# A hybrid decoder layer: triangular inverses on GpSimd, sums of squares in ScalarE's copies, two evacuations on ScalarE

## The chip, the core and the metric

The kernel runs on one core of one Trainium2 chip. The core's engines work beside each other, each through its own queue in order: TensorE (PE in the profile; its weight loads are PEld), VectorE (DVE), ScalarE (ACT), GpSimd (POOL) and SyncE (SP), which here issues the DMAs. The metric is the device time of one execution, in microseconds (us), as the median of several runs.

## What is computed

A layer over 16 meta tokens and 512 tokens of width 1024. RMS normalisation, one wide projection, and then two branches that run side by side: eight heads of differential softmax attention, and eight heads of a gated DeltaNet in chunks. Both are normalised, gated, projected, merged and projected again. What the change touches, cut from the reference:

```python
m = where(strict, einsum(kb, k) * decay, 0.0)                 # per head and chunk
t_inv = triangular_solve(m + eye, eye, lower, unit_diagonal)  # its inverse
v_new = u_c - w_c @ state                                     # u, w come from t_inv
o_c   = qd_c @ state + a_c @ v_new
state = state * cd_c + kd_c.T @ v_new
o_d   = rms_norm(o_d, dn_norm_w)
...
p  = softmax(where(causal, s, -inf))
pd = p[:, :, 0] - lam * p[:, :, 1]
o_a = rms_norm(pd @ v, attn_norm_w) * (1 - lam_init)
```

The kernel takes chunks of 128 tokens for the DeltaNet, and the 16 meta tokens as a first state.

## The kernel before

**The order is planned.** The program is written as many small tasks (Python generators) that say `yield ENGINE` before the instructions for that engine, `yield ("pool",)` where they need a buffer and `yield "event"` where they wait for another task. The class `Plan` (lines 82 to 192) plays the tasks through at build time with a charge for every instruction (`Engine.time`, lines 224 to 251) and for every hop between engines, takes the task that could start first, by rank where two are equal, and so fixes the order of the instructions in every engine's queue. On the chip each engine takes its queue strictly in that order and waits where an input is late. For GpSimd the plan charges `100 + 2.2 * n` nanoseconds for a two-input instruction of n elements per partition that isn't a power (line 250), and no gap between two of them that depend on each other; for VectorE `69 + n / 0.96` and a gap of 130 between dependent ones.

**TensorE's work.** The dense products (`product`, line 737) multiply the normalised tokens, split in two float32r parts (hnH, hnL), with blocks of 128 columns of weights, split likewise (wh, wl): 8 blocks of 128 rows by three passes, over 512 columns, or over two pieces of 272 and 256. Each block of weights is loaded (SP: `raw`), rounded by ACT (`wh`) and its rest taken by DVE (`wl<-raw,wh`, 128x1024, both inputs in SBUF). These products are rank 4 in the plan and fill every place that the heads leave.

**The DeltaNet heads** go in four groups of two (`delta_pair`, line 900). Per group: the products of keys with keys and with queries (lines 1040 and 1041; rows `kT` and `qT,kT` of PE), which DVE scales into MT and AT. The 32x32 diagonal blocks of MT go through DRAM (`scrm`) into msub, where one partition holds one block: 32 blocks of the two heads and one of the meta tokens, twice, in 97 partitions. There the inverse is built by substitution in 31 steps (lines 1166 to 1173), each of two dependent instructions: `tmps<-msub,ts` (a product) and `ts<-ts,tmps` (a difference) on n = 31 - j rows by w = min(j + 1, 16) columns. The result goes through DRAM (`scrt`) to td, and PE takes it up in the row `td,MT` (line 1258), the first of a chain that assembles the inverse TT of 128x128 (`square`), and then runs the four chunks (`steps`, line 1318). PE's queue holds dense products between the last `qT,kT` row of a group and its first `td,MT` row: while the inverse is under way, these keep PE busy.

**The attention heads** (`attention`, line 1405) run in the same stretches: scores into psc, row maxima on DVE, exponentials on ACT, the combination `e<-e,ast,e` on DVE (both inputs in SBUF), transposes into PSUM, copies into pT, the product with the values, and the norm.

**The sums of squares** of the norms: after all four chunks of a head are copied out of PSUM by ACT, ACT squares the 128x512 tile (lines 1372 and 1520) and DVE reduces it (1374 and 1522). **The values** of the DeltaNet are transposed into PSUM, and DVE scales all four chunks in one instruction into vr (line 1001). **The transposed softmax weights** are copied into pT by ACT in every second block of queries and by DVE in the others (lines 1444 to 1449).

GpSimd does little: the masks of E, clearing ts and TT, powers of a few elements, and the DMAs that move half of the keys to other partitions (`ak<-ak`).

## Time and profile before

| | |
|---|---|
| median of 3 runs | 784.66 us (784.42 to 785.24) |
| the profiled execution, its own time | 781.76 us |
| its span, first to last instruction | 780.1 us |
| granted TensorE clock, mean | 0.996 |
| busy: PE, DVE, ACT, POOL | 752.1, 601.7, 410.6, 76.1 us |

The profile is one execution. The page gives the busy time of each engine, the costliest groups of instructions and what ended their waits. `bank<-hnH,wh` is an instruction that writes the PSUM tile bank and reads hnH and wh; nearly all instructions carry one line number, that of the helper that records them, so they are told apart by tiles. The view of waits says which engine waited for which, in total, how often, and longest. The view of stretches gives each engine's busy time between two moments, and the granted clock of TensorE. The timeline lists instructions by start and duration; in brackets stands how long the engine had been idle and what ended that.

### The profile page before, as it was taken

What the parts mean: (1) busy time and instruction counts of PE and PEld (TensorE: products, weight loads), DVE (VectorE), ACT (ScalarE), POOL (GpSimd) and SP (SyncE); (2) the same over time, 40 slices, a digit from 0 to 9 for tenths busy, and PEclk for the clock granted to TensorE, in tenths of its full rate; (3) what the DMA queues carried; (4) which work ended last, traced back from release to release, by engine and by line L of the source; (5) the groups of instructions that cost most, each with busy time, mean ns of one, the idle gap of its engine ahead of it and who ended that gap; (6) DMA issues with size and microseconds to landing.
All of it is one profiled execution on the core that took longest, in us unless ns stands there. A gap on an engine that the chain in (4) does not pass through costs nothing.

```text
span 780.1 us, 14350 instructions
## 1 busy us (share of the span) xinstructions
PE 752.1 (96%) x5479; PEld 688.9 (88%) x5479; DVE 601.7 (77%) x1415; ACT 410.6 (53%) x1000; POOL 76.1 (10%) x114
## 2 busy tenths in 40 slices
PE   5999999999999999998999999899999999999996
PEld 5999878999988899987899998788988998899886
DVE  6788698688669678868967884995697887879643
ACT  5374535676544557654466744355565445545332
POOL 4120002021100201100030201001000000000001
PEclk9999999999999999999999999999999999999999
DMA  8032624212352500254250125223022332332802
GB/s 311 33 110 82 156 82 101 69 38 83 85 153 83 124 29 28 82 143 96 82 123 29 55 84 125 85 86 93 28 82 82 108 110 84 105 101 89 271 0 109
DMA packets 46749, 74.43 MB, mean 95 GB/s; under 512 B 20528, under 2 KB 29136, under 8 KB 46680
## 3 DMA queue, kind: packets, MB, share of 16 engines
q1 hardware_dynamic: 45400, 69.18, 29.0%
q0 software_dynamic: 1280, 4.33, 2.7%
q8 instruction: 43, 0.70, 0.4%
q14 instruction: 26, 0.21, 0.1%
HBM read 65.98 MB, written 3.19 MB: 89 GB/s over the span
## 4 chain that ended last, share of the span: by engine, by line
PE 41%; DMA 4%; DVE 4%; ACT 2%; issue 1%; POOL 1%; SPq 1%; POOLq 0%; ACTq 0%; DVEq 0%
PE bank L220 39%; PE psc L220 1%; DMA msub<-scrm 1%; DMA scrt<-ts 1%; DVE wl L220 1%; DVE ts L220 1%; SPq L220 1%; DVE tmps L220 1%; DMA eg<-gcd 1%; DMA raw<-in_wout_dram 1%; DMA td<-scrt 0%; POOL ts L220 0%; DVE aq L220 0%; ACT wh L220 0%; DVE MT L220 0%
## 5 line engine op out<-in xcount | busy, mean ns | idle before, releaser
L220 PE MATMUL bank<-hnH,wh 128*128 128x512 f32 (+3 forms) x944 | 317.0, 338 | 0.8 <-ACT hnH L220 0.8
L220 PE MATMUL bank<-hnH,wl 128*128 128x512 f32 (+3 forms) x944 | 302.4, 322 | 3.2 <-DVE wl L220 3.2
L220 PE MATMUL bank<-hnL,wh 128*128 128x512 f32 (+3 forms) x944 | 301.8, 322 | 0.0
L220 PEld LDWEIGHTS bank<-hnH,wl 128*128 128x128 f32 x944 | 177.3, 189 | 19.0 <-DVE wl L220 5.1
L220 PEld LDWEIGHTS bank<-hnH,wh 128*128 128x128 f32 x944 | 177.4, 189 | 13.4 <-ACT hnH L220 1.0
L220 PEld LDWEIGHTS bank<-hnL,wh 128*128 128x128 f32 x944 | 177.8, 189 | 10.4
L220 DVE TENSOR_TENSOR wl<-raw,wh 128x1024 fp32r<-128x1024 f32 x82 | 100.1, 1220 | 22.6 <-ACT wh L220 22.2
L220 ACT CAST wh<-raw 128x1024 fp32r<-128x1024 f32 x82 | 85.9, 1048 | 40.8 <-PE bank L220 29.9
L220 DVE SCALAR_TENSOR_TENSOR y<-xp,pc,y 128x528 f32<-128x528 f32 (+1 forms) x72 | 54.2, 754 | 0.8 <-ACT y L220 0.2
L220 ACT ACTIVATE e<-psc,ast 128x144 f32<-128x144 f32 (+3 forms) x64 | 34.5, 541 | 31.8 <-DVE ast L220 27.8
L220 DVE TENSOR_TENSOR tmps<-msub,ts 97x240 f32<-97x240 f32 (+27 forms) x124 | 39.2, 316 | 4.6 <-DMA msub<-scrm 2.9
L220 DVE TENSOR_TENSOR ts<-ts,tmps 97x240 f32<-97x240 f32 (+27 forms) x124 | 39.4, 318 | 1.8
L220 PE MATMUL bank<-btH,Wh 128*128 128x256 f32 x128 | 36.1, 282 | 1.6 <-ACT sn L220 1.6
L220 PE MATMUL bank<-btL,Wh 128*128 128x256 f32 x128 | 35.7, 279 | 0.0
L220 PE MATMUL bank<-btH,Wl 128*128 128x256 f32 x128 | 35.7, 279 | 0.0
L220 PE MATMUL psc<-ak,aq 128*128 128x264 f32 (+3 forms) x160 | 29.1, 304 | 5.8 <-ACT e L220 5.8
L220 PEld LDWEIGHTS psc<-ak,aq 128*128 128x128 f32 x160 | 23.6, 189 | 8.7 <-ACT e L220 7.5
L220 DVE TENSOR_TENSOR Wl<-raw,Wh 128x1024 fp32r<-128x1024 f32 (+1 forms) x24 | 24.8, 1042 | 7.2 <-ACT Wh L220 7.0
L220 ACT CAST Wh<-raw 128x1024 fp32r<-128x1024 f32 (+1 forms) x24 | 21.5, 905 | 16.7 <-DVE raw L220 5.6
L220 POOL DMA_DIRECT2D ak<-ak x16 | 8.8, 551 | 219.6 <-DVE ak L220 160.9
L220 DVE TENSOR_REDUCE ast<-psc 128x1 f32<-128x528 f32 (+3 forms) x40 | 28.4, 710 | 0.2
L220 PEld LDWEIGHTS bank<-btH,Wh 128*128 128x128 f32 x128 | 24.0, 188 | 2.6 <-ACT sn L220 2.2
(339 smaller groups left out, 1466.6 us busy)
## 6 DMA issues: line engine op xcount, KB each, us to landing
raw<-in_wblk_dram SPq DMA_DIRECT2D x96, 512.0 KB, 3.5
ak<-ak POOLq DMA_DIRECT2D x16, 264.0 KB, 4.3
raw<-in_wout_dram SPq DMA_DIRECT2D x8, 512.0 KB, 4.2
xt<-in_x_dram SPq DMA_DIRECT2D x4, 512.0 KB
E<-gcd SPq DMA_DIRECT2D x8, 256.0 KB, 5.0
eg<-gcd SPq DMA_DIRECT2D x8, 256.0 KB
xr<-in_x_dram SPq DMA_DIRECT2D x8, 256.0 KB, 6.8
out_dram<-xr SPq DMA_DIRECT2D x8, 256.0 KB, 2.3
```

Source lines behind the costliest of these rows:

```text
L220: return real(*args, **kw)
```

## The change

Four parts. The 62 instructions of each group's inverse are issued on GpSimd. The squares of the DeltaNet's and the attention's outputs are taken chunk by chunk by ACT straight from PSUM, each behind the copy of the same chunk, with ACT's accumulator giving the sum: the two large squares and the two reduces per head go. The values are scaled by four ACT instructions instead of one of DVE. All copies into pT are ACT's. The memory reserved for descriptors of GpSimd's DMAs is halved, from 4096 to 2048.

```diff
-            yield DVE
-            V.tensor_tensor(out=vr[i], in0=pt, in1=sc[:, i, :, vs_].unsqueeze(2).broadcast_to([P, NC, P]), op=ALU.mult)
+            for c in range(NC):
+                yield ACT
+                A.activation(out=vr[i][:, c, :], in_=pt[:, c, :], func=AF.Copy, scale=sc[:, i, c, vs_:vs_ + 1])
...
         for j in range(31):
             n, w = 31 - j, min(j + 1, 16)
-            yield DVE
+            yield POOL
             tm = mk(dp, [P, 256], F32, "tmps", 2)[0:97, 0:n * w].rearrange("p (i c) -> p i c", c=w)
-            V.tensor_tensor(out=tm, in0=msub[0:97, j, j + 1:32].unsqueeze(2).broadcast_to([97, n, w]),
+            G.tensor_tensor(out=tm, in0=msub[0:97, j, j + 1:32].unsqueeze(2).broadcast_to([97, n, w]),
                             in1=ts_[0:97, j, 0:w].unsqueeze(1).broadcast_to([97, n, w]), op=ALU.mult)
-            yield DVE
-            V.tensor_tensor(out=ts_[0:97, j + 1:32, 0:w], in0=ts_[0:97, j + 1:32, 0:w], in1=tm, op=ALU.subtract)
+            yield POOL
+            G.tensor_tensor(out=ts_[0:97, j + 1:32, 0:w], in0=ts_[0:97, j + 1:32, 0:w], in1=tm, op=ALU.subtract)
...
                     A.copy(out=o[:, c, :], in_=pk[:, 3 * P:4 * P])
+                    A.activation(out=mk(dp, [P, P], F32, "sqk", 1), in_=pk[:, 3 * P:4 * P], func=AF.Square,
+                                 accum_out=co[:, c:c + 1])
                     give("pdl", pk)
...
-            A.activation(out=sq, in_=o, func=AF.Square)
-            yield DVE
-            V.tensor_reduce(out=co, in_=sq, axis=AX.X, op=ALU.add)
...
-            if i % 2:
-                yield ACT
-                A.copy(out=dst, in_=pt[:, :w])
-            else:
-                yield DVE
-                V.tensor_copy(out=dst, in_=pt[:, :w])
+            yield ACT
+            A.copy(out=dst, in_=pt[:, :w])
...
             A.copy(out=o[:, i, :], in_=po[:, 0:P])
+            A.activation(out=mk(ap, [P, P], F32, "sqo", 1), in_=po[:, 0:P], func=AF.Square, accum_out=ss[:, i:i + 1])
             give("pat", po)
...
-        sq = slot(ap, [P, L], F32, "e")[:, :SEQ].rearrange("p (c d) -> p c d", d=P)
-        ss = mk(ap, [P, NC], F32, "ass", 2)
-        yield ACT
-        A.activation(out=sq, in_=o, func=AF.Square)
-        yield DVE
-        V.tensor_reduce(out=ss, in_=sq, axis=AX.X, op=ALU.add)
...
-    nc = _bacc.Bacc("TRN2", target_bir_lowering=False, num_devices=1, dynamic_dma_scratch_size=4096)
+    nc = _bacc.Bacc("TRN2", target_bir_lowering=False, num_devices=1, dynamic_dma_scratch_size=2048)
```

Since the plan sees other charges, the order changes on every engine from the first group on. Three places matter for what follows.

GpSimd's queue where the first group's inverse stands. Before, the mask of E follows the moves of the keys, and then the next tile ts is cleared:

```order
L220 DMA ak_1031<-ak_1031 64x1056 x2
L220 AFFINE_SELECT E_1018<-E_1018 128x512
L220 AFFINE_SELECT E_1085<-E_1085 128x512
L220 DMA ak_1602<-ak_1602 64x1056
L220 MEMSET ts_1605 64x512
L220 AFFINE_SELECT ts_1605<-ts_1605 64x512
```

Now the 62 instructions of the inverse stand there without a break. The first of them:

```order
L220 AFFINE_SELECT E_998<-E_998 128x512
L220 DMA ak_1038<-ak_1038 64x1056
L220 TENSOR_TENSOR tmps_1159<-msub_108,ts_648 97x31
L220 TENSOR_TENSOR ts_648<-ts_648,tmps_1159 97x31
L220 TENSOR_TENSOR tmps_1163<-msub_108,ts_648 97x60
L220 TENSOR_TENSOR ts_648<-ts_648,tmps_1163 97x30x2
```

And the last of them, with what is queued behind: the second mask of E, the clearing of ts and TT, the moves of the next attention head's keys, and the power of the first attention head's norm.

```order
L220 TENSOR_TENSOR tmps_1547<-msub_108,ts_648 97x16
L220 TENSOR_TENSOR ts_648<-ts_648,tmps_1547 97x16
L220 AFFINE_SELECT E_1095<-E_1095 128x512
L220 MEMSET ts_1558 64x512
L220 AFFINE_SELECT ts_1558<-ts_1558 64x512
L220 MEMSET ts_1558 64x512
L220 AFFINE_SELECT ts_1558<-ts_1558 64x512
L220 MEMSET TT_1563 128x1024
L220 MEMSET t_246_1564 32x8x32
L220 DMA ak_1604<-ak_1604 64x1056 x2
L220 TENSOR_TENSOR ass_1282<-ass_1282,mhalf 128x4
```

The mask moved behind the inverse; the moves and the power were there behind the clearing before, too.

VectorE's queue in the middle of the same inverse. Before, its steps alternate with the attention's rows:

```order
L220 TENSOR_TENSOR ts_648<-ts_648,tmps_1311 97x18x14
L220 SCALAR_TENSOR_TENSOR od_132<-th_1309,bank_5_82 128x512
L220 TENSOR_TENSOR tmps_1337<-msub_108,ts_648 97x255
L220 TENSOR_TENSOR psc_1332<-psc_1332,amask 128x2x128
L220 TENSOR_TENSOR ts_648<-ts_648,tmps_1337 97x17x15
L220 TENSOR_REDUCE ast_1322<-psc_1332 128x2
```

Now only the others are left, among them the rest of the weights (wl) and the combination e, whose two inputs both lie in SBUF:

```order
L220 TENSOR_SCALAR ast_1283<-ast_1283 128x2
L220 TENSOR_TENSOR wl_1303<-raw_1051,wh_1302 128x1024
L220 SCALAR_TENSOR_TENSOR od_132<-th_1317,bank_2_79 128x512
L220 RECIPROCAL ast_1283<-ast_1283 128x1
L220 SCALAR_TENSOR_TENSOR ast_1283<-ast_1283,nlam,l_182_1281 128x1
L220 SCALAR_TENSOR_TENSOR e_1284<-e_1285,ast_1283,e_1284 128x144
```

Between a group's first and last inverse step VectorE has four `wl` rows in the first three groups and five in the last, and three `e` rows in each.

TensorE's queue at the first `td,MT` row. Before, it is row 616, and the last `qT,kT` row of the group is row 311:

```order
L220 MATMUL bank_6_83<-hnH,wh_1525 128x256
L220 MATMUL bank_6_83<-hnL,wh_1525 128x256
L220 MATMUL bank_6_83<-hnH,wl_1526 128x256
L220 MATMUL bank_1_78<-td_1606,MT_955 32x32 x4
L220 MATMUL bank_1_78<-td_1606,MT_999 32x32 x4
```

Now it is row 551, and the last `qT,kT` row is row 311 again:

```order
L220 MATMUL bank_2_79<-hnH,wh_1487 128x512
L220 MATMUL bank_2_79<-hnL,wh_1487 128x512
L220 MATMUL bank_2_79<-hnH,wl_1488 128x512
L220 MATMUL bank_6_83<-td_1559,MT_936 32x32 x4
L220 MATMUL bank_6_83<-td_1559,MT_1028 32x32 x4
```

So fewer dense products stand between the two, in each of the four groups. Counted in the two orders, by columns:

| dense rows between the last `qT,kT` and the first `td,MT` | before: 512, 272, 256 | now: 512, 272, 256 |
|---|---|---|
| group 1 | 138, 72, 72 | 123, 48, 48 |
| group 2 | 141, 90, 72 | 138, 48, 48 |
| group 3 | 141, 72, 57 | 135, 48, 48 |
| group 4 | 141, 72, 57 | 117, 48, 48 |

The number of PE's rows in the whole program is the same, 4230: what is missing there stands elsewhere.

More of the change, by code (lines that the diff above doesn't have):

```diff
@@ L1325, in steps @@
             k, q, o = pair["k", h], pair["q", h], mt[i]
-            state = S_[i]
+            state, co = S_[i], mk(dp, [P, NC], F32, "co", 2)
             for c in range(NC):
@@ L1369, in steps @@
             yield f"qe{h}"
-            sq, co = vr[i], mk(dp, [P, NC], F32, "co", 2)
-            yield ACT
-            A.activation(out=sq, in_=o, func=AF.Square)
-            yield DVE
-            V.tensor_reduce(out=co, in_=sq, axis=AX.X, op=ALU.add)
             give("vr")
@@ L1411, in attention @@
         o, l0 = slot(ap, [P, NC, P], F32, "ao"), mk(ap, [P, NC], F32, "l0", 2)
+        ss = mk(ap, [P, NC], F32, "ass", 2)
         def scores(dst, i, m, c0, w):
@@ L1515, in attention @@
         give("vs")
-        yield ("e",)
-        sq = slot(ap, [P, L], F32, "e")[:, :SEQ].rearrange("p (c d) -> p c d", d=P)
-        ss = mk(ap, [P, NC], F32, "ass", 2)
-        yield ACT
-        A.activation(out=sq, in_=o, func=AF.Square)
-        yield DVE
-        V.tensor_reduce(out=ss, in_=sq, axis=AX.X, op=ALU.add)
-        give("e")
         yield DVE
```

## The prediction

> **What bounds the kernel now.** I read the page first, then who waits on PE, then the stretches in which the inverses run.

> ```profile
> PE 752.1 (96%) x5479; PEld 688.9 (88%) x5479; DVE 601.7 (77%) x1415; ACT 410.6 (53%) x1000; POOL 76.1 (10%) x114
> ```

> ```profile
> PE psc L220 <- ACT e L220: 5.8, 4, 1.9
> PE bank L220 <- DVE wl L220: 3.2, 4, 1.3
> PE bank L220 <- DMA td<-scrt: 1.8, 2, 1.1
> ```

> PE is busy for all but 28 us of the span. The waits that a different order can touch are these three: for the exponentials, whose row maxima come from a crowded DVE; for the rest of a weight block; and for the inverse (td). PE's own work stays as it is, so the change acts through PE's waits alone. Now the stretches from a group's first inverse step to its `td,MT` row on PE (first of four and their sum; the columns are length and the busy time of PE, PEld, DVE, ACT and POOL), and then the inverses alone, first of four and sum:

> ```profile
> 89.59:136.07 46.48, 44.54 (x265) 38.68 (x264) 41.44 (x115) 21.45 (x52) 5.05 (x7) 0.96 0.33 92
> ...
> sum 181.38, PE 171.32 PEld 149.66 DVE 161.32 ACT 87.02 POOL 15.88; mean PE 42.83 PEld 37.41 DVE 40.33 ACT 21.76 POOL 3.97
> ```

> ```profile
> 89.59:127.95 38.36, 36.42 (x204) 30.96 (x203) 35.97 (x106) 16.42 (x42) 1.25 (x1) 0.96 0.27 93
> ...
> sum 146.68, PE 138.42 PEld 118.75 DVE 140.94 ACT 66.52 POOL 1.88; mean PE 34.60 PEld 29.69 DVE 35.23 ACT 16.63 POOL 0.47
> ```

> PE idles 181.38 - 171.32 = 10.06 us in the four stretches; that is all that a freer DVE and a quicker inverse can win there. The four inverses take 146.7 us, 36.7 each, on a DVE that is 96% busy. And PE's queue fits them closely. In groups 1 and 3 the inverse reached PE (DVE takes td up at the same time) shortly before PE came to it; in 2 and 4 PE waited, the 1.8 us above.

> ```profile
> 134.91 0.45 DVE L220 STREAM_TRANSPOSE tdt<-td 128x256 f32<-128x256 f32 x1 [0.94 <-DMA td<-scrt]
> 136.07 1.00 PE L220 MATMUL bank<-td,MT 32*32 32x32 f32 x29
> ```

> ```profile
> 398.62 0.45 DVE L220 STREAM_TRANSPOSE tdt<-td 128x256 f32<-128x256 f32 x1 [0.67 <-DMA td<-scrt]
> 399.94 1.00 PE L220 MATMUL bank<-td,MT 32*32 32x32 f32 x29
> ```

> The slack is 1.16 and 1.32 us, 2.5 in all. So the length of the inverse and the dense work placed beside it decide.

> **The change part by part.** *The cover.* The counts of dense rows before `td,MT` fall by 15, 3, 6, 24 of 512 columns, by 24, 42, 24, 24 of 272, and by 24, 24, 9, 9 of 256. What a row costs PE I read from start to start:

> ```profile
> 208.54 0.40 PE L220 MATMUL bank<-hnH,wl 128*128 128x512 f32 x1
> ...
> 209.93 0.39 PE L220 MATMUL bank<-hnH,wl 128*128 128x512 f32 x1
> ```

> ```profile
> 201.09 0.29 PE L220 MATMUL bank<-hnH,wl 128*128 128x272 f32 x1
> ...
> 202.22 0.29 PE L220 MATMUL bank<-hnH,wl 128*128 128x272 f32 x1
> 202.35 0.28 PE L220 MATMUL bank<-hnH,wh 128*128 128x256 f32 x1
> ...
> 203.62 0.28 PE L220 MATMUL bank<-hnH,wl 128*128 128x256 f32 x1
> ```

> Six steps of 512 in 1.39 us are 0.232 each, nine of 272 in 1.13 are 0.126, eleven of 256 in 1.27 are 0.115. That is 48 x 0.232 + 114 x 0.126 + 66 x 0.115 = 11.1 + 14.4 + 7.6 = 33.1 us of cover less. This work isn't gone; it stands elsewhere, where PE is already busy. (A few small transposes move too; I leave them out.)

> *The inverse on POOL.* The trace of before has no two-input arithmetic on POOL but powers of a few elements, so I bound it by POOL's one-input rows: 128 elements, 512 in one run, and 512 in runs of 16.

> ```profile
> L220 POOL TENSOR_SCALAR_AFFINE_SELECT upper<-ones 128x128 f32<-128x128 f32 x1 | 0.3, 295 | 0.0
> ```

> ```profile
> 356.05 0.63 POOL L220 TENSOR_SCALAR_AFFINE_SELECT E<-E 128x512 f32<-128x512 f32 x1 [8.74 <-ACT E L220]
> ```

> ```profile
> 133.14 0.84 POOL L220 TENSOR_SCALAR_AFFINE_SELECT ts<-ts 64x512 f32<-64x512 f32 x1
> 134.03 0.52 POOL L220 MEMSET ts<- 64x512 f32 x1
> ```

> From 0.295 to 0.63 over 384 elements is 0.87 ns an element, with 0.183 us fixed; runs of 16 make it (0.84 - 0.183) / 512 = 1.28 ns; and the next instruction starts 0.05 us after the end (134.03 after 133.98). A group has 62 instructions with 9,552 elements: twice the sum of (31 - j) x min(j + 1, 16). Fixed parts and gaps: 62 x 0.233 = 14.5 us. The elements: at least 9,552 x 0.87 ns = 8.3 us, if two operands stream like one; at twice that 16.6; at twice the rate of short runs 24.5. So 22.8, 31.1 or 39.0 us. I take the middle one, since nothing shows that POOL reads two operands in the time of one, and only the smaller steps have short runs.

> On top comes the port. When POOL read SBUF beside DVE instructions with two inputs in SBUF, each kept the other out:

> ```profile
> 90.95 1.22 DVE L220 TENSOR_TENSOR wl<-raw,wh 128x1024 fp32r<-128x1024 f32 x1
> 92.08 0.68 DVE L220 TENSOR_TENSOR ts<-ts,tmps 97x87 f32<-97x87 f32 x1
> ```

> ```profile
> 91.41 1.25 POOL L220 TENSOR_SCALAR_AFFINE_SELECT E<-E 128x512 f32<-128x512 f32 x1 [7.04 <-ACT E L220]
> ```

> ```profile
> 133.26 0.72 DVE L220 TENSOR_TENSOR pm<-e,pm 128x16 fp32r<-128x16 f32 x1
> ```

> ```profile
> L220 DVE TENSOR_TENSOR pm<-e,pm x32: 151/166/717, 111.7 to 584.0; 128x16 fp32r<-128x16 f32 x32
> ```

> The mask of E began at 91.41 in the middle of a wl (90.95 to 92.17) and took 1.25 instead of 0.63 us; the small step of DVE behind (0.68) ended with it. At 133.26 a pm of usually 0.166 us took 0.72, until POOL's mask of ts was over at 133.98. So the inverse on POOL stands still while DVE runs such an instruction. A group's inverse now has at least four wl and three e beside it:

> ```profile
> L220 DVE TENSOR_TENSOR wl<-raw,wh 128x1024 fp32r<-128x1024 f32 x82 | 100.1, 1220 | 22.6 <-ACT wh L220 22.2
> ```

> ```profile
> L220 DVE SCALAR_TENSOR_TENSOR e<-e,ast,e x32: 355/563/771, 108.3 to 582.9; 128x144 f32<-128x144 f32 x8, 128x272 f32<-128x272 f32 x8, 128x400 f32<-128x400 f32 x8, 128x528 f32<-128x528 f32 x8
> ```

> 4 x 1.22 + 3 x 0.56 = 6.6 us, from nothing (if they fall into POOL's gaps) to all of it; I take 5.9. The inverse becomes 31.1 + 5.9 = 37.0 us, with 22.8 and 45.6 as the ends. That is about what it takes now; it loses DVE's queue and gains slower arithmetic.

> *The rest.* ACT gets 64 small squares and 32 scalings and loses 16 large squares, and takes 16 more copies:

> ```profile
> L220 ACT ACTIVATE sqk<-bank 128x128 f32<-128x128 f32 x64 | 17.8, 278 | 9.4 <-PE bank L220 8.3
> ```

> ```profile
> L220 ACT ACTIVATION_READ_ACCUMULATOR sqk<-bank 128x1 f32 x64 | 12.7, 198 | 0.0
> ```

> 64 x (0.278 + 0.198) is 30 us more at most, on an engine that is 53% busy over the whole span; each square holds its PSUM bank 0.5 us longer, which PE's dense rows cover; without that cover it would be 0.5 us per chunk of a head. I cost these, the scalings and the copies at nothing: what they take off DVE is a part of the 10.06 us, and that stays hidden as long as PE ends up waiting for td. The smaller descriptor memory too: the sixteen moves are the same, and behind the inverse they come when PE waits anyway.

> *The sum.* Where PE waits for td, the other waits in the stretch are swallowed, and a group costs: new inverse minus old, minus slack, plus the dense work that it no longer hides. For four: 4 x 37.0 - 146.7 - 2.5 + 33.1 = +31.9 us. A wait also costs clock:

> ```profile
> 103.99 0.77 PE L220 MATMUL psc<-ak,aq 128*128 128x272 f32 x4 [1.91 <-ACT e L220]
> ```

> ```profile
> 105.00:106.00 1.00, 1.00 (x4) 0.81 (x3) 1.00 (x3) 0.00 (x0) 0.00 (x0) 0.50 0.34 66
> ```

> After 1.91 us without work PE ran at a clock of 0.50, from about 104.4 to 108: some 3.5 us at half speed, 1.75 lost. Four waits instead of that one: +5.25. In all +37.2, against the profiled execution's 781.76 us: 819.0. The median stands 2.9 higher, so **821.9 us**. In short: median + 4 x inverse - 110.9.

> **The rivals.** *The inverse fits its cover.* If POOL takes two operands as fast as one and DVE's instructions fall into its gaps, it lasts 22.8 to 26.5 us and PE never waits: (146.7 + 2.5 - 33.1 - 10.06) / 4 = 26.5 is the point. Then up to 10.06 us are won: 774.6 us. [...] Between 26.5 and 29.0 us lies no change.

> *Only a part of it.* One-operand rate with the full port wait: 22.8 + 6.6 = 29.4 us; gaps of the clock may stay away. This gives 785 to 806 us up to 33 us.

> *POOL is slower still.* At the rate of short runs and the full wait, 45.6 us: 784.66 + 182.4 - 110.9 = 856 us. For it: the early steps have runs of one to eight elements. Against it: half of the elements are in runs of 16. [...]

> *PE waits at another place.* If POOL's lock delays wl, PE waits for weights before td; but then td comes later in PE's queue by as much, and the sum holds.

> **How the numbers follow.** Inverse of 33 to 41 us (806 to 838 us): 0.50. Longer (838 to 856): 0.17. 29 to 33 us (785 to 806): 0.12. It fits (774.6 to 783.1): 0.17. Within 0.2%, which is about what a measurement of this kernel can tell from no change: 0.04. So faster 0.17, slower 0.79. The range leaves out the last third of the fast case and the top of the slow one: 778 to 852 us.

> **What would show it.** In the new profile: inverses of about 37 us on POOL, PE waiting 5 to 12 us before `td,MT` four times, and a clock near 0.5 after each; steps of about 0.18 us + 1.74 ns an element where no wl runs beside, and longer by a wl where one does; PE's waits for psc and wl mostly gone. I am wrong if POOL's steps run at 1 ns an element or below, or if PE does not wait for td. I am wrong in the cover if PE waits although the inverse is under 29 us.

## The result and the profile after

The changed kernel takes 838.26 us (median of 4 runs, 836.96 to 842.13), the kernel before 784.54 (4 runs); the ratio is 1.0698, with a 95% interval of 1.0656 to 1.0739. It is slower by 7%, and the forecast was 821.9, with a range of 778 to 852. The profiled execution of the changed kernel is the longest of its four (842.13 us), that of before (781.76) was shorter than its median, so the two profiles differ by 60.4 us and the medians by 53.7.

The page of the changed kernel, first part, and PE's two largest waits:

```profile
PE 766.7 (91%) x5479; PEld 698.2 (83%) x5479; DVE 537.0 (64%) x1127; ACT 431.2 (51%) x1160; POOL 215.4 (26%) x362
```

```profile
PE bank L220 <- DMA td<-scrt: 54.6, 4, 15.3
PE bank L220 <- ACT sq L220: 7.9, 1, 7.9
```

All of the loss can be read from these lines. PE's idle time is the span less its busy time: 840.4 - 766.7 = 73.7 us, against 28.0 before, so 45.7 more. Its busy time is up by 14.6 us on the same 5479 instructions. Together that is 60.3 us, the whole difference of the spans. The four waits for td are the only new idle time of any size; the waits for the exponentials (5.8 us before) are gone, and of those for wl one of 1.5 us is left (3.2 us before). DVE's queue is 65 us shorter, and it helps nothing.

The stretches from the first step of an inverse to its `td,MT` row (the four, and the sum; length, then busy time of PE, PEld, DVE, ACT, POOL, and the granted clock):

```profile
92.88:139.13 46.25, 31.03 (x176) 25.87 (x176) 21.44 (x40) 18.52 (x53) 37.44 (x67) 0.90 0.23 64
241.67:288.48 46.81, 34.09 (x191) 28.30 (x189) 23.01 (x42) 18.48 (x52) 37.50 (x67) 0.91 0.23 64
387.17:433.85 46.68, 33.94 (x191) 28.20 (x189) 22.83 (x41) 18.36 (x52) 37.37 (x66) 0.89 0.23 63
534.21:580.75 46.54, 31.19 (x187) 26.64 (x186) 19.47 (x37) 16.22 (x49) 35.99 (x64) 0.89 0.22 64
sum 186.28, PE 130.24 PEld 109.02 DVE 86.76 ACT 71.58 POOL 148.30; mean PE 32.56 PEld 27.25 DVE 21.69 ACT 17.89 POOL 37.08
```

The stretches are hardly longer than before (186.28 against 181.38 us), but PE works in 130.24 us of them instead of 171.32. DVE, which was 96% busy while it did the inverses, is now busy for less than half of the time: it was not what PE lacked. The first inverse on GpSimd in the timeline, its first and last instruction, and PE's row behind it:

```profile
92.88 1.04 POOL L220 TENSOR_TENSOR tmps<-msub,ts 97x31 f32<-97x31 f32 x1 [9.72 <-DMA msub<-scrm]
...
132.22 0.22 POOL L220 TENSOR_TENSOR ts<-ts,tmps 97x16 f32<-97x16 f32 x1
```

```profile
139.13 1.73 PE L220 MATMUL bank<-td,MT 32*32 32x32 f32 x32 [14.10 <-DMA td<-scrt]
```

The four inverses take 39.56, 40.07, 39.93 and 39.65 us, 159.2 in all and 39.8 each (36.7 before, 37.0 forecast). From the end of an inverse to PE's row lie 6.7 to 6.9 us of trips through DRAM. The steps of GpSimd, two subtractions and two products, beside which DVE runs nothing or only rows that don't hold them up (a reduction, a small scaling; in the fit below they hold GpSimd up for 0.02 and -0.08 of the time beside it):

```profile
119.02 0.67 POOL L220 TENSOR_TENSOR ts<-ts,tmps 97x224 f32<-97x224 f32 x1
131.60 0.25 POOL L220 TENSOR_TENSOR ts<-ts,tmps 97x32 f32<-97x32 f32 x1
...
118.37 0.57 POOL L220 TENSOR_TENSOR tmps<-msub,ts 97x224 f32<-97x224 f32 x1
131.28 0.24 POOL L220 TENSOR_TENSOR tmps<-msub,ts 97x32 f32<-97x32 f32 x1
```

A subtraction costs 0.42 us for 192 elements more, 2.19 ns each, a product 1.72, both with 0.18 us fixed, and the next starts 0.08 us after the end. (The 114 of 248 steps that have no DVE instruction beside them lie within 0.008 us of these two straight lines in the mean; the longest subtractions, of 231 and 255 elements, are 0.04 to 0.05 us quicker than theirs.) For 62 steps and 2 x 4,776 elements that is 62 x 0.26 + 4,776 x 3.91 ns = 34.8 us. The rest, 5 us, is DVE's doing:

```profile
107.67 1.54 DVE L220 TENSOR_TENSOR wl<-raw,wh 128x1024 fp32r<-128x1024 f32 x1 [1.58 <-ACT wh L220]
```

```profile
108.21 1.57 POOL L220 TENSOR_TENSOR ts<-ts,tmps 97x240 f32<-97x240 f32 x1
```

A subtraction of 240 elements, by the line 0.71 us, took 1.57 beside a wl, and the wl 1.54 instead of 1.22. Over all 248 steps the excess above the lines is 20.6 us. Divided among the DVE instructions beside them by least squares, a wl holds GpSimd up for 0.77 of the 26.3 us in which the two overlap (20.2 us), and e for none of its 12.7 us.

Last, the clock. PE without work from 125.03 to 139.13, and what it is granted (the third number from the right; the first two rows lie in the wait, the others 7 to 9 us behind its end, with PE at work):

```profile
130.00:131.00 1.00, 0.00 (x0) 0.00 (x0) 0.00 (x0) 0.00 (x0) 0.76 (x4) 0.65 0.00 0
131.00:132.00 1.00, 0.00 (x0) 0.00 (x0) 0.00 (x0) 0.00 (x0) 0.77 (x4) 0.50 0.00 0
...
146.00:147.00 1.00, 1.00 (x3) 0.33 (x1) 0.13 (x1) 0.00 (x0) 0.01 (x1) 0.50 0.58 122
147.00:148.00 1.00, 1.00 (x15) 0.81 (x16) 0.00 (x0) 0.06 (x1) 0.00 (x0) 0.82 0.80 156
148.00:149.00 1.00, 1.00 (x49) 0.96 (x45) 0.00 (x0) 0.40 (x3) 0.00 (x0) 1.00 0.03 8
```

From 130.3 to 147.4 the clock is 0.50, 17.1 us, of which PE works 8.2. Read from the trace, the four waits bring 17.1, 13.7, 23.9 and 17.1 us at half clock. What PE loses by it while it is at work, half of that time, is 4.1, 2.8, 6.9 and 3.5 us: 17.4 in all, against 1.7 in the kernel before. That is the 14.6 us of busy time, and a little more.

### The profile page after: what moved, and what is told of

It is laid out like the page before. It is cut to its first block, busy times and chain, and to the rows that moved or that the text cites. A ratio compares the mean times of both kernels' runs of the same rounds, so it can differ in the third digit from the quotient of the medians.

```text
span 840.4 us, 14469 instructions
## 1 busy us (share of the span) xinstructions
PE 766.7 (91%) x5479; PEld 698.2 (83%) x5479; DVE 537.0 (64%) x1127; ACT 431.2 (51%) x1160; POOL 215.4 (26%) x362
## 3 DMA queue, kind: packets, MB, share of 16 engines
q1 hardware_dynamic: 45400, 69.18, 26.5%
## 5 line engine op out<-in xcount | busy, mean ns | idle before, releaser
L220 PE MATMUL bank<-hnH,wh 128*128 128x512 f32 (+3 forms) x944 | 323.7, 345 | 0.8 <-ACT hnH L220 0.8
L220 PE MATMUL bank<-hnH,wl 128*128 128x512 f32 (+3 forms) x944 | 304.9, 325 | 1.5 <-DVE wl L220 1.5
L220 PE MATMUL bank<-hnL,wh 128*128 128x512 f32 (+3 forms) x944 | 304.6, 325 | 0.0
L220 PEld LDWEIGHTS bank<-hnH,wl 128*128 128x128 f32 x944 | 179.4, 191 | 16.4 <-DVE wl L220 1.9
L220 PEld LDWEIGHTS bank<-hnH,wh 128*128 128x128 f32 x944 | 179.6, 191 | 16.0 <-issue 1.7
L220 PEld LDWEIGHTS bank<-hnL,wh 128*128 128x128 f32 x944 | 180.1, 192 | 10.1
L220 DVE TENSOR_TENSOR wl<-raw,wh 128x1024 fp32r<-128x1024 f32 x82 | 103.6, 1263 | 34.2 <-ACT wh L220 34.1
L220 ACT CAST wh<-raw 128x1024 fp32r<-128x1024 f32 x82 | 86.0, 1049 | 50.2 <-PE bank L220 45.9
L220 POOL TENSOR_TENSOR ts<-ts,tmps 97x240 f32<-97x240 f32 (+27 forms) x124 | 76.6, 618 | 9.7
L220 POOL TENSOR_TENSOR tmps<-msub,ts 97x240 f32<-97x240 f32 (+27 forms) x124 | 63.5, 512 | 28.6 <-DMA msub<-scrm 19.2
L220 PE MATMUL bank<-td,MT 32*32 32x32 f32 x128 | 6.9, 237 | 54.6 <-DMA td<-scrt 54.6
L220 DVE SCALAR_TENSOR_TENSOR y<-xp,pc,y 128x528 f32<-128x528 f32 (+1 forms) x72 | 54.5, 757 | 1.6 <-ACT y L220 0.7
L220 PEld LDWEIGHTS bank<-td,MT 32*32 32x32 f32 x128 | 6.4, 150 | 56.4 <-DMA td<-scrt 56.4
L220 POOL TENSOR_TENSOR ssq<-ssq,mhalf 128x1 f32<-128x1 f32 x4 | 3.4, 852 | 175.0 <-DVE ssq L220 175.0
L220 ACT ACTIVATE e<-psc,ast 128x144 f32<-128x144 f32 (+3 forms) x64 | 34.6, 544 | 10.2 <-DVE ast L220 9.8
L220 DVE STREAM_TRANSPOSE tdt<-td 128x256 f32<-128x256 f32 x4 | 1.8, 446 | 56.9 <-DMA td<-scrt 56.9
L220 PE MATMUL bank<-btH,Wh 128*128 128x256 f32 x128 | 36.1, 282 | 1.7 <-ACT sn L220 1.7
L220 ACT COPY TT<-tdt 32x256 f32<-32x256 f32 x16 | 6.4, 402 | 60.0 <-POOL TT L220 27.4
L220 PE MATMUL bank<-btL,Wh 128*128 128x256 f32 x128 | 35.7, 279 | 0.0
L220 PE MATMUL bank<-btH,Wl 128*128 128x256 f32 x128 | 35.7, 279 | 0.0
L220 POOL TENSOR_TENSOR ass<-ass,mhalf 128x4 f32<-128x4 f32 x8 | 8.2, 1023 | 104.8 <-DVE ass L220 104.8
L220 DVE TENSOR_TENSOR psc<-psc,amask 128x256 f32<-128x256 f32 (+1 forms) x40 | 15.0, 375 | 27.8 <-PE psc L220 27.4
```

Source lines behind the costliest of these rows:

```text
L220: return real(*args, **kw)
```

## The experiments

Three theories stand against each other. **A**: GpSimd is a little slower than DVE in this place, but the loss comes from the order. The planner charges an inverse 62 x 100 + 2.2 x 9,552 = 27.2 us, the chip takes 39.8, so the order puts about 12 us too little dense work beside each, and each wait costs clock as well. **B**: the added work on ScalarE costs something; **C**: GpSimd is the wrong place whatever the order. The runs of before that each is compared with ran on the same chip (medians 783.0 to 784.8 us).

**One part alone: only the inverse.** The kernel before, with this edit:

```diff
-            yield DVE
+            yield POOL
...
-            V.tensor_tensor(out=tm, in0=msub[0:97, j, j + 1:32].unsqueeze(2).broadcast_to([97, n, w]),
+            G.tensor_tensor(out=tm, in0=msub[0:97, j, j + 1:32].unsqueeze(2).broadcast_to([97, n, w]),
```

(and the same for the subtraction).

> The kernel before with one edit: the 62 instructions of each inverse are issued on GpSimd; sums of squares, values and softmax copies stay as before. Theory A (the inverse on GpSimd, with too little dense work placed beside it, is the whole loss): the dense rows beside the four inverses are worth 157.2 us by the row durations, 8.1 less than in the full change (165.3), so PE waits about 8 us longer for td than the 54.6 us there: 838.3 + 8 = 846 us (840 to 852). Rival B (the added work on ScalarE, which holds PSUM banks longer, carries a good part of the loss): clearly less than the full change, below 830 us.

Measured: 849.85 us, ratio 1.0834 (1.0797 to 1.087). The inverse alone brings the whole loss and 11.6 us more. The total is in theory A's range, but not for its reason, which was 8 us more of waiting for td: PE waits as long for td as in the full change, and the difference is made of other waits.

```profile
PE bank L220 <- DMA td<-scrt: 54.9, 4, 15.7
...
PE bank L220 <- ACT pmT L220: 4.5, 4, 1.3
PE bank L220 <- DVE ao L220: 4.2, 3, 2.2
PE bank L220 <- DVE wl L220: 2.9, 2, 2.0
```

**The other parts alone: all but the inverse.** The full change with `POOL` and `G` set back to `DVE` and `V` in the two steps.

> The full change with the inverse put back on VectorE: squares with accumulation, scaled values and softmax copies on ScalarE stay, and the smaller descriptor memory. Theory A: no loss; cover for the inverse is 192.3 us against 198.3 before, the inverse shortens since VectorE has fewer instructions beside it: 780 us (775 to 788), PE waits for td under 5 us in all. Rival B: above 795 us, with new waits of PE for PSUM banks.

Measured: 786.25 us (12 runs), ratio 1.003 (0.9994 to 1.0066): no difference. PE's idle time in its profile is 785.2 - 752.7 = 32.5 us, and its waits for td are 1.5:

```profile
PE bank L220 <- DMA td<-scrt: 1.5, 3, 1.1
```

Rival B is out. The inverse was expected to shorten; it hardly did: 144.4 us for the four, 146.7 before.

**The order with the chip's price.** The full change, with one number of the planner altered:

```diff
-            return 300 + 164 * n if kw["op"] == ALU.pow else 100 + 2.2 * n
+            return 300 + 164 * n if kw["op"] == ALU.pow else 340 + 1.95 * n
```

> The full change with one number of the planner altered: a two-input instruction on GpSimd is charged 340 + 1.95 n ns instead of 100 + 2.2 n, so that an inverse is charged 39.7 us (measured 39.8) instead of 27.2. The order then places 210.9 us of dense rows beside the four inverses, 45.6 more. Theory A: PE's waits for td fall from 54.6 to about 9 us, the clock loss from 14.6 to about 5: 838.3 - 45.6 - 9.6 = 783 us (778 to 795). Rival C (GpSimd is too slow for this place, whatever the order; the dense work is then missing elsewhere): the waits move to other places and the time stays above 815 us.

Measured: 808.97 us, ratio 1.0327 (1.0286 to 1.0369). More than half of the loss goes with one number of the planner, on the same instructions, so C, which asked for more than 815 us, is out as it stands; but 783 was too low. Where the rest went, by PE's waits, the clock behind the first of them and SyncE's queue:

```profile
PE bank L220 <- DMA td<-scrt: 14.4, 4, 4.1
```

```profile
142.00:143.00 1.00, 0.00 (x0) 0.00 (x0) 0.00 (x0) 0.00 (x0) 0.89 (x3) 0.96 0.54 87
143.00:144.00 1.00, 0.21 (x4) 0.21 (x5) 0.23 (x1) 0.00 (x0) 0.93 (x2) 0.50 0.83 114
...
155.00:156.00 1.00, 1.00 (x6) 1.00 (x6) 0.04 (x1) 0.60 (x1) 0.00 (x0) 0.50 0.00 0
156.00:157.00 1.00, 1.00 (x7) 0.85 (x7) 0.03 (x1) 0.98 (x4) 0.00 (x0) 0.71 0.00 0
```

```profile
132.97 0.95 SPq L220 DMA_DIRECT2D scrt<-ts  x1
134.01 1.70 SPq L220 DMA_DIRECT2D raw<-in_wblk_dram  x1
135.76 0.84 SPq L220 DMA_DIRECT2D scrt<-ts  x1
141.40 0.39 SPq L220 DMA_DIRECT2D td<-scrt  x1
```

The waits fell from 54.6 to 14.4 us. They did not go: the inverses grow to 41.5 to 42.3 us, and PE's row comes 9.2 to 10.9 us behind the end of an inverse instead of 6.7 to 6.9. The likely reason is that with the dense work come its weights, with more wl rows for DVE, and with a load of 512 KB that now stands in SyncE's queue between the inverse's way into DRAM and its way back (in the first group, shown here, between its two writes). And the clock cost did not fall at all: the waits of 2.6 to 4.1 us bring 6.8 or 13.7 us at half clock, nearly all of it at work, 18.6 us lost.

**Does PE's longer busy time come from the clock?** In the full change, ahead of PE's `td,MT` rows:

```diff
+        for r in range(54):
+            nc.tensor.matmul(px[:, 0:512], hn[0][:, r % KB, 0:P], hn[0][:, r % KB, 0:512], start=True, stop=True)
```

> The full change with useless work: before each group's first td,MT row PE does 54 dense matmuls of 512 columns on tokens (their result is overwritten), about 12.5 us at full clock, in the time in which it otherwise waits 12.6 to 15.3 us. Theory A with its clock term (PE's busy time grew by 14.6 us, 766.7 - 752.1, since PE runs at a clock of 0.5 for 5 to 14 us behind each long wait): the clock stays at 1, and although PE has 50 us more work, the time falls by 10 to 14 us, to 826 us (823 to 830). Rival D (the 14.6 us are something else, such as slower products next to GpSimd's traffic): 838 us or more, PE's clock as in the full change.

Measured: 826.88 us, 11.4 less than the full change, with 50 us more work on PE.

```profile
123.18 12.61 PE L1258 MATMUL bank<-hnH 128*128 128x512 f32 x54
137.56 1.09 PE L220 MATMUL bank<-td,MT 32*32 32x32 f32 x32 [1.77 <-DMA td<-scrt]
```

Useless work makes the kernel faster, since it keeps the clock up: what is lost at half clock falls from 17.4 to 5.1 us, and 12.3 is about what the time falls by. Rival D is out. Two waits of over 1 us are left, of 1.77 and 1.98 us, and even they are followed by 3.4 and 6.8 us at half clock.

**The same where only short waits are left.** The kernel with the charge of 340, and 14 such matmuls instead of 54.

> As with the planner's charge of 340 + 1.95 n, and 14 useless dense matmuls of 512 columns (3.2 us) on PE before each group's first td,MT row, where it waited 2.6 to 4.1 us. Theory A2 (the clock loss is a fee per wait of more than about 2 us, hardly dependent on its length: PE's busy time was 14.6 us up with four waits of 14 us and is 16.4 us up with four waits of 4 us): the waits left are under 1 us each, the clock stays at 1 behind them, and the time falls by about 16 us, from 809 to 793 (788 to 797). Rival D (the clock loss is in proportion to the time without work, or the busy time is up for another reason): within 4 us of 809.

Measured: 797.19 us, the median of four runs (790.18, 792.80, 801.57 and 807.28), 11.8 less than with the charge alone; the ratio to the kernel before, taken without the longest run, is 1.0137 (1.0073 to 1.0202). Rival D (within 4 us of 809) is out, and of theory A2 only half holds: the profile, that of the run of 801.57, still shows a wait for td of 1.92 us, followed by 17.1 us at half clock, and one of 1.85 us for ao, followed by 3.4; 9.8 us are lost instead of 18.6. So the cost is a fee per wait that hardly depends on its length, but it isn't the same for each wait. Nor for each run: in the order above, the mean clock granted to the four runs is 0.996, 0.996, 0.985 and 0.977, and what is missing from 1, times the span, is 3.2, 3.2, 12.0 and 18.5 us. That is 15.3 of the 17.1 us that lie between the quickest run and the longest.

**More cover.** Charges of 380 + 1.95 n and 420 + 1.95 n:

> The full change with a charge of 380 + 1.95 n ns: 225.8 us of dense rows beside the four inverses, 14.9 more than with 340, which left waits for td of 14.4 us and the clock fees of four waits. Theory A2: the waits fall to about nothing, and the fees with them: 808 - 14 - 16 = 778 us (774 to 788), about 1% faster than the kernel before. Rival C2 (each further weight block placed there brings its VectorE instruction, which holds up GpSimd, and its 512 KB load, which stands in SyncE's queue between the inverse's two trips through DRAM, so that td comes later by as much): waits of 2 to 4 us stay, 800 us or more.

> The full change with a charge of 420 + 1.95 n ns: 235.8 us of dense rows beside the four inverses, 24.9 more than with 340. Theory A2: no waits for td, no clock fees: 778 us (772 to 788). Rival C2: waits of 2 us or more stay, 800 us or more. Rival E (the dense rows are now used up too early and PE waits where they were before, on DVE's and ScalarE's hops in the chunks): no waits for td, but over 790 us, with new waits of PE.

Measured: 784.70 us, ratio 0.9995 (0.9971 to 1.0019), and 783.91 us, ratio 1.0001 (0.9975 to 1.0028). Both take as long as the kernel before, so C is out for good: with enough work beside it, GpSimd is no worse a place. With 380 two waits for td are left (2.81 and 1.52 us):

```profile
PE bank L220 <- DMA td<-scrt: 4.3, 2, 2.8
```

With them and a wait of 1.75 us for um, 11.9 us are lost at half clock. The time lies in A2's range, but the fees that A2 said would go are still there; the 800 us of C2 are far off. With 420 no wait for td is left, and the loss at half clock is 1.7 us as in the kernel before:

```profile
PE 758.6 (97%) x5479; PEld 690.1 (88%) x5479; DVE 539.1 (69%) x1127; ACT 430.6 (55%) x1160; POOL 226.0 (29%) x362
```

For 420 theory A2 said 778, rival C2 waits of 2 us or more, rival E over 790 with new waits. None has it: the td waits are gone and PE's idle time is 782.1 - 758.6 = 23.5 us, 4.5 less than before; but its busy time is 6.5 us more, at the same clock and with the same work. Taken from the starts of all its rows, 4.1 of that lie behind the rows `vin,TT` and `S,kT` of the chunks (16.4 us from each to the next row's start, waits left out, 12.3 before), where fewer dense rows now stand between the steps: from a group's first `S,kT` row to its last `u,ktd` row 129 in the four groups, 216 before. So E has the place right, and overrated the price. These pauses are too short for the view of waits.

**Does DVE hold GpSimd up?** Two experiments, one run each. First, with wl copied from wh, so that only one input is read (this kernel leaves out the low parts of the weights):

```diff
-        V.tensor_tensor(out=wl, in0=raw, in1=wh.bitcast(F32), op=ALU.subtract)
+        plan.spend(DVE, V.time("tensor_tensor", (), dict(out=wl, in0=raw, in1=wh)))
+        nc.vector.tensor_copy(out=wl, in_=wh)
```

> The full change, but the instruction that takes the rest of a weight block reads one input instead of two (a copy of wh into wl, so the low parts of the weights are left out); the planner is charged the same, so that the order is the same. Theory L (a two-input VectorE instruction on SBUF and an instruction of GpSimd keep each other out): GpSimd's steps beside wl are no longer held up by about 1 us, the inverses fall from 39.8 to about 36 us, PE's waits from 54.6 to about 40, the time to about 823 us. Rival M (any VectorE instruction slows GpSimd in proportion to its length, as two users of one memory): a copy shortens only by its own length, inverses of 38 us or more.

Measured: 824.53 us; inverses of 36.4, 37.3, 37.1 and 36.9 us, waits for td of 44.1 us. The time is as expected, the reason isn't quite: the copy holds GpSimd up too.

```profile
104.95 0.82 DVE L401 CAST wl<-wh 128x1024 fp32r<-128x1024 f32 x1 [1.71 <-ACT wh L220]
```

```profile
105.30 0.95 POOL L220 TENSOR_TENSOR tmps<-msub,ts 97x247 f32<-97x247 f32 x1
106.33 0.68 POOL L220 TENSOR_TENSOR ts<-ts,tmps 97x247 f32<-97x247 f32 x1
```

The product, by the line 0.61, took 0.95. By the same fit the copies hold GpSimd up for 0.48 of the time beside it, and they are shorter (0.82 us in the row of DVE above, 1.22 or more for a wl). So neither L (no hold-up) nor M (38 us or more) is right; the figure lies between. By what means a wl or a copy holds GpSimd up, no run here tells. For e, an instruction with two inputs in SBUF as well, the price falls on the other side. In the kernel before and in the changed kernel:

```profile
108.31 0.36 DVE L220 SCALAR_TENSOR_TENSOR e<-e,ast,e 128x144 f32<-128x144 f32 x1
```

```profile
103.44 0.76 DVE L220 SCALAR_TENSOR_TENSOR e<-e,ast,e 128x144 f32<-128x144 f32 x1
```

```profile
103.46 0.57 POOL L220 TENSOR_TENSOR tmps<-msub,ts 97x207 f32<-97x207 f32 x1
104.11 0.60 POOL L220 TENSOR_TENSOR ts<-ts,tmps 97x207 f32<-97x207 f32 x1
```

GpSimd's steps take about what the lines give (0.54 and 0.63), and e takes 0.76 us instead of 0.36: here DVE pays, although e began first.

Second, with wl done twice:

```diff
+        nc.vector.tensor_tensor(out=wl, in0=raw, in1=wh.bitcast(F32), op=ALU.subtract)
```

> The full change, with VectorE's instruction for the rest of a weight block done twice (the same result again; the planner isn't charged for it, so that the order is the same). In the full change such an instruction of 1.22 us or more holds up GpSimd's steps for 0.77 of the time in which they overlap, about 0.95 us for each of five in an inverse. Theory L: twice as many hold it up twice: 4.7 us more in each inverse, 44.5 us instead of 39.8; PE's waits for td grow from 54.6 to about 73 us and the time by 19 to about 857 us (850 to 862). Rival M2 (GpSimd gets in between the two, and is held up only once): inverses under 42 us, time under 848.

Measured: inverses of 43.4 to 45.0 us, 44.2 in the mean, as theory L has it (44.5). Each of the two wl holds up a step (by the lines 0.33 and 0.37 us):

```profile
103.06 1.20 POOL L220 TENSOR_TENSOR tmps<-msub,ts 97x87 f32<-97x87 f32 x1
104.33 1.22 POOL L220 TENSOR_TENSOR ts<-ts,tmps 97x87 f32<-97x87 f32 x1
```

```profile
102.72 1.34 DVE L220 TENSOR_TENSOR wl<-raw,wh 128x1024 fp32r<-128x1024 f32 x1
104.09 1.23 DVE L401 TENSOR_TENSOR wl<-raw,wh 128x1024 fp32r<-128x1024 f32 x1
```

But the time is 883.99, not 857: wl stands on PE's own path as well. PE's waits for td are no longer than in the full change (51.7 us), and many small ones for DVE and ScalarE come on top (in the first 95 us 3.5 us for ss and 2.4 for y, 0.5 and none in the full change); PE takes longer over the same cover, so td is no later for it. That was left out of the expectation.

**Cover, but only the inverse.** The kernel before with the inverse on GpSimd and a charge of 420 + 1.95 n, then 450 + 1.95 n; and the full change with 450:

> The kernel before with two edits: the inverse on GpSimd, and the planner's charge of 420 + 1.95 n ns for its instructions; 226.1 us of dense rows beside the four inverses (235.8 in the full change with this charge, which took as long as the kernel before). Theory A2: with enough cover, no waits for td over 2 us, and about the time before: 786 us (781 to 792); the other edits then matter little either way. Rival B (with the sums of squares and the copies still on VectorE and held up by GpSimd, PE's waits for VectorE grow): 795 us or more.

> The kernel before with the inverse on GpSimd and a charge of 450 + 1.95 n ns: 239.3 us of dense rows beside the inverses, 13.2 more than with 420, whose profile still had one wait for td of 1.4 us and 6.8 us lost to a half clock behind it. Theory A2: that wait and its fee go, nothing else changes: 776 us (773 to 781), faster than the kernel before by about 1%. Rival E (dense rows taken here are missing between the steps of the chunks, where PE then pays small hops): same as with 420, 782 to 786 us.

> The full change with a charge of 450 + 1.95 n ns: 242.1 us of dense rows beside the inverses, 6.3 more than with 420, which had no wait for td left. Theory A2 and rival E agree that no wait is left to remove; A2 (more cover costs nothing): 784 us as with 420; rival E (each us of cover too many costs hops in the chunks): 786 to 790 us.

Measured: 782.82 us, ratio 0.9987 (0.9963 to 1.0011); 782.23 us, ratio 0.9975 (0.9947 to 1.0002); 780.65 us, ratio 0.9963 (0.9938 to 0.9988). The first two are no different from the kernel before. With 420 A2 has the time (786, B asked for 795 or more); with 450 it said 776, and rival E, with 782 to 786, is nearer: the one wait for td in the profile with 420 and the half clock behind it did go, but they had cost so much in some runs only (the clock granted to the twelve is 0.990 to 0.999). The last kernel lies 0.4% below the one before, and is the only one whose interval leaves out 1 on that side; its page:

```profile
PE 757.3 (97%) x5479; PEld 688.7 (88%) x5479; DVE 542.3 (70%) x1127; ACT 432.8 (56%) x1160; POOL 227.4 (29%) x362
```

PE's idle time is 778.8 - 757.3 = 21.5 us, and no wait for td is over 0.5. Its inverses take 40.7 to 42.1 us, 5 more than on DVE, and cost nothing. Neither A2 nor E had expected the full change to take less than with 420, and with 87 dense rows between the steps of the chunks it should by E have taken more; why 450 is better (busy time 757.3 against 758.6, idle time 21.5 against 23.5) wasn't followed further, and one order more or less at this distance proves little.

## Why the prediction was right, and where its sizes were off

The time lies in the range, 16.4 us above the forecast, and the mechanism was as forecast. PE waits for td four times, each wait costs clock, the waits for the exponentials vanish beneath them, DVE's relief is worth nothing there, and the other three edits cost nothing (786.25 us without the inverse on GpSimd). The waits are longer than the 5 to 12 us that were named as the sign: 12.6 to 15.3 us.

**The inverse** was put at 31.1 us plus 5.9 for the port, the forecast's name for the time that DVE's instructions cost GpSimd, and measures 34.8 plus 5.0. Both choices (twice the masks' price for an element, 1.74 ns; 0.05 us between steps) were a little low: 1.95 ns in the mean and 0.08 us. That is 4 x 2.8 = 11.2 us of the gap. The subtractions take 2.19 ns an element by the two rows shown, 1.97 by a fit to all 56 that stand alone; the products are quicker (1.72). The bound of 41 us in the forecast's chances no run shows; measured are 39.8 us an inverse. By the forecast's sum 41 us give 838. That this is the measured time is luck in part: the inverses took 1.2 us less each, and the clock cost 10.5 us more than in that sum.

**The port** came out at the right size with a wrong list, which is luck: nearly all of it is wl (20.2 of 20.6 us in the four inverses); e was counted too, and it is e that waits (0.76 us instead of 0.36).

**The cover** held. With the measured inverses the sum gives 159.2 - 146.7 - 2.5 + 33.1 = 43.1 us of waiting beyond the 10.1 that PE idled there before, 53.2; the waits are 54.6.

**The clock** was the term that failed most: four waits of 1.75 us each, 5.25 more than before, were forecast, since the one wait of the old trace had cost that. Measured are 17.4 - 1.7 = 15.7. A fee of 3.5 us at half clock was taken to be the same for every wait; it is one step of a fee that runs up to seven, the wait's own part included.

With these two corrected, 821.9 + 11.2 + 10.5 = 843.6 us, against 842.13 in the profiled execution and 838.26 in the median (the forecast started from a profiled execution that was 2.9 below its median and added that; here the profile lies above).

**The rivals.** "It fits its cover" asked for an inverse under 26.5 us, and fell with the rate. (By the forecast's own sum, inverses of 26.5 to 29.0 us would have won between 10 us and nothing, where it says no change.) "Slower still" has it half right: the subtractions run near its rate (2.56 ns an element), the products do not, and 39.8 us lies between the forecast's 37.0 and its 45.6. What none of them said is what the charge runs show: the cover isn't given, but follows from the planner's price for GpSimd. The prediction took the order as it stood, which was right for this kernel, and saw no more in it than a count of rows.

## What to carry to other kernels

Where a planner fixes the order, an operation that moves to another engine moves with its price: compare the price with the chip's before judging the engine. Here 27.2 us charged against 39.8 taken went with a loss of 54 us. The right price gave back 29 of them, and with an allowance on top (380 to 450 ns for each instruction instead of 340) the same instructions cost nothing. They gained next to nothing either, since the engine they left was hardly what PE waited for. When a busy engine waits, count the work beside the wait as well as the wait, and look at the clock behind it.

## What the runs showed of the hardware

```profile
274.71 1.17 PE L220 MATMUL bank<-td,MT 32*32 32x32 f32 x29 [1.37 <-DMA td<-scrt]
```

```profile
276.00:277.00 1.00, 1.00 (x6) 0.79 (x4) 0.92 (x5) 0.65 (x2) 0.53 (x2) 0.50 0.12 49
288.00:289.00 1.00, 1.00 (x7) 0.78 (x6) 0.65 (x1) 0.17 (x1) 0.00 (x0) 0.50 0.00 0
```

With charges of 420 and 450 in the full change, 3.4 us of half clock even followed pauses of 0.98 us and less. Over the steps of the grid: in the one just before a stretch at half clock, PE was busy for 0 to 78% of the time; but steps with as little as 46% were followed by the full clock.

One step with PE at work did not always end the half clock. PE, by its rows at work all the time, got the full clock back only after as many as five (17.1 us behind a wait of 1.52, in the full change with a charge of 380). All 35 stretches ended with a step in which PE was busy throughout, but 23 such steps did not end theirs, and 14 of these held 16 or more rows of 32x32 or 64x64 blocks, where none of the 35 held more than 11. Whether those small rows are the reason, no run here tells; for the other nine no reason shows.
